# Late modulation blocks in the sample's small PSUM banks, and the sample's rows four partitions to a row

## The chip, the cores and the metric

The kernel runs on one core of one Trainium2 chip. The metric is device time in microseconds (us) of one execution, lower is better. Five engines work side by side: PE (TensorE, matrix products; PEld is its weight load), DVE (VectorE), ACT (ScalarE), POOL (GpSimd) and SP, whose queue issues nearly all direct DMAs here.

## The reference, cut to what matters

One inference step of a one-layer decoder over 512 prompt rows and 32 sample rows (8 sequences of 4). Both groups use the same weights:

```python
def adaln_mods(c, w_ada, b_ada):
    m = (jax.nn.silu(c) @ w_ada + b_ada)[:, None, :]
    return jnp.split(m, 6, axis=-1)

def finish(x, att, y_ssm, mods, g_att_out, w_out, g_norm2, ...):
    mixed = jnp.concatenate([rmsnorm(att, g_att_out), y_ssm], axis=-1) @ w_out
    x = x + mods[2] * mixed
    h = rmsnorm(x, g_norm2) * (1 + mods[4]) + mods[3]
    return x + mods[5] * hier_moe(h, w_rg, b_rg, w_re, b_re, w_gate, w_up, w_down)
```

`w_ada` is 1024 x 6144; its columns make the six modulations of 1024 columns each. Ahead of `finish` stand the input projection, three attention branches (compressed, selected, window) and a Mamba scan, each for prompt and sample. The model width is 1024; the mixture has 16 experts, two per row.

## The kernel before, in words

The kernel is written on a tile framework. A tile is taken from a pool by a tag; a tag has a fixed number of buffers, and a new tile of the tag takes the place of an older one once that one's readers are done. [...] `in_turn` (L360) only ties the PE instructions of the blocks that it wraps to one another, in the order in which they were traced.

The stage that the first half of the change touches is that of PSUM pool `pp2` (L850): tag `s` (scores, one pair of banks), `pt` (two banks; turns and evacuations of the prompt's attention), `ot` (one, attention output), `sm` (two) and `smo` (one) for the sample. In the order of the text:

- `win_half(0)`, compressed attention and top-k ranks of the sample, `sel_first(0)`: the first of two halves of selected attention for sample batches 0 to 3. `attend(t, br)` (L871) is attention of one prompt tile of 128 rows in branch `br`; it takes `s`, `pt` and `ot`. `attend(0, 1)`, `sel_second(0)`, `attend(1, 1)`, `win_half(1)` (L1240 to L1245).
- The sample's Mamba step, L1247 to L1362: turns, `hst` (the state) through four pairs of `sm` tiles (L1283 to L1294), `pe`, `pw_`, `pseg`, `py`, `pz`, and so on. Nearly every product goes to an `sm` bank.
- `sel_first(1)`, `attend(0, 0)`, `attend(2, 1)`, `sel_second(1)` (L1364 to L1367).
- The late blocks, L1377: `in_turn(ada_block, n, late_rows(n), "pt")` for n = 8 to 11. `ada_block` (L293) multiplies 512 columns of `w_ada` by the nine conditioning rows (32 columns of stationary data) into one bank, 64 PE records and 8 for the bias, and copies the bank to `mods`. `late_rows` (L1369) loads the block's 2 MB in two DMAs on SP's queue into the two buffers of tag `wt`, which `win_half(1)` used before. Then `store_mods(4, 8)` (L305) writes the four blocks to DRAM.
- `attend(3, 1)` (L1380), the prompt's compressed attention (L1382 to L1431, all of its PSUM tiles `pt`), `attend(1, 0)`, `attend(2, 0)`, `attend(3, 0)`.

The next stage (pool `pp3`, from L1456) turns the attention output (L1533), multiplies by `w_out` and keeps the 32 sample rows as 32 partitions x 1024 columns: `mixS`, `xs1`, and the three modulations `m0S`, `a2S`, `m3S`, each read back from DRAM (`mod_rowS`, L1505, a DMA that repeats every row four times). `samp_out` (L353) copies a bank of four 32-row blocks (partitions 32 j, columns 128 j) in four pieces to `mixS` (L1688). `sample_rows` (L1667) squares, norms, modulates, stores to `h2d` and runs the router in two halves (`router`, L1619). `OSEQ` (L30) is the order: 'm0 s f0 m1 r0 f1 m2 r1 f2 f3 m3 r2 r3', with s for `sample_rows`, m for a product tile of 128 prompt rows, f and r for its norm and router. After it come 17 expert tiles.

Of the kernel before, what the change touches and what calls it, by code (L numbers as in the profile page):

```python
# [9 lines left out]
F32 = mybir.dt.float32  # L10
# [9 lines left out]
KC = 8  # L20
# [30 lines left out]
def hybrid_step(ctx: ExitStack, tc: tile.TileContext, a, o):  # L51
# [21 lines left out]
    def W(pl, shape, dt, tag, bufs=2):  # L73
        return pl.tile(list(shape), dt, name=nm(tag), tag=tag, bufs=bufs)
# [10 lines left out]
    def PS(tag="ps"):  # L85
        return psum["pool"].tile([P, 512], F32, name=nm(tag), tag=tag, bufs=psum["tags"][tag])
# [7 lines left out]
    def mm(out, lhsT, rhs, start=True, stop=True):  # L94
        T.matmul(out, lhsT, rhs, start=start, stop=stop)  # L95
# [209 lines left out]
    def store_mods(n0, n1):  # L305
        for j in range(4):
            SP.dma_start(modd[:, n0:n1, j, :], mods[32 * j:32 * j + 9, n0:n1, :])
# [45 lines left out]
    def samp_out(ps, n, dst):  # L353
        for j in range((n + P - 1) // P):
            e = min(n, (j + 1) * P)
            dst(ps[32 * j:32 * j + 32, 0:e - j * P], j * P, e)
# [3 lines left out]
    def in_turn(f, *args):  # L360

        traced = nc.cur_bb.bb.instructions
        n0 = len(traced)
        r = f(*args)
        for i in traced[n0:]:
            if i.engine == mybir.EngineType.PE:
                if tail[0] is not None:
                    tc.add_manual_dep(i, tail[0].name, mybir.DependencyInfo(mybir.DependencyClass.NoSync,
                                                                            mybir.DependencyReason.DATA),
                                      reason="in_turn")  # L370
                tail[0] = i
        return r

    def proj(pl, H, L, lhs, w, n, dst, nb=2, ks=range(KC), between={}):

        acc = [PS("acc") for _ in range(NT)]
        ps = PS() if lhs is not None else None
        parts = {}  # L380
        turn = in_turn if between else lambda f, *args: f(*args)

        def prod(t, k):
            wh, wl = parts[k]
            sl = slice(t * P, (t + 1) * P)
            mm(acc[t][:, 0:n], H[:, k, sl], wh, start=k == ks[0], stop=False)
            mm(acc[t][:, 0:n], H[:, k, sl], wl, start=False, stop=False)
            mm(acc[t][:, 0:n], L[:, k, sl], wh, start=False, stop=k == ks[-1])

        for i, k in enumerate(ks):  # L390
            parts[k] = split_w(pl, w(k), n, nb)
            if i <= KC - nb:
                for t in range(NT):
                    turn(prod, t, k)
            if lhs is not None and i % 4 == 3:
                for j in ks[i - 3:i + 1]:
                    turn(samp_k, ps, lhs, w(j), n, j, ks)
            for f in between.get(k, ()):
                f()
        for t in range(NT):  # L400
            for k in ks[KC - nb + 1:]:
                turn(prod, t, k)
        if lhs is not None:
            samp_out(ps, n, dst)
        return acc

    def to_us(col):
# [359 lines left out]
    def CS(shape, dt, name):  # L767
        return smp.tile(list(shape), dt, name=name, tag=name)

    with tc.high_priority(offset=-2500):  # L770
# [33 lines left out]
                        teq[:, None, None, :].to_broadcast([P, 2, 8, 4]), op=OP.mult)  # L804
        X4 = CS([64, 64, 4], BF, "X4")
        V.tensor_copy(X4, ident[0:64, 0:64, None].to_broadcast([64, 64, 4]))
        sel32 = CS([P, 32], F32, "sel32")
        V.tensor_reduce(sel32, ident.rearrange("p (j r) -> p r j", r=32), axis=AX.X, op=OP.add)
        Eb = CS([P, 32, 8], BF, "Eb")
        V.tensor_copy(Eb, sel32[:, :, None].to_broadcast([P, 32, 8]))  # L810
# [102 lines left out]
    def C3(shape, dt, name):  # L913
        return W(p3, shape, dt, name, 1)
# [181 lines left out]
    def sel_first(hb, gt):  # L1096
        mx0, sm0, po = sel_part(hb, 0, gt)
        mx0_ = W(p3, [P, 1], F32, "mx0")
        V.tensor_copy(mx0_, mx0)
        po0 = W(p3, [P, P], F32, "pdT")  # L1100
        V.tensor_copy(po0, po[:, 0:P])
        return mx0_, sm0, po0

    def sel_second(hb, gt, mx0_, sm0, po0):
        mx1, sm1, po1 = sel_part(hb, 1, gt)
        mn = W(p3, [P, 1], F32, "mxm")
        V.tensor_tensor(mn, mx0_, mx1, op=OP.min)
        e0 = W(p3, [P, 1], F32, "e0")
        S.activation(e0, mx0_, AF.Exp, scale=-1.0, bias=mn)
        e1 = W(p3, [P, 1], F32, "e1")  # L1110
        S.activation(e1, mx1, AF.Exp, scale=-1.0, bias=mn)
        V.tensor_mul(sm0, sm0, e0)
        V.scalar_tensor_tensor(sm0, sm1, e1, sm0, op0=OP.mult, op1=OP.add)
        cf = factor(hb, 1, sm0)
        V.tensor_mul(e0, e0, cf)
        V.tensor_mul(e1, e1, cf)
        add_rows(hb, po0, e0)
        add_rows(hb, po1, e1)
# [125 lines left out]
    attend(1, 1, True)  # L1244
    win_half(1, wt1)  # L1245

    dtaS = C3([NS, 8], F32, "dtaS")  # L1247
    V.tensor_mul(dtaS, dtS, nega[0:NS])

# [30 lines left out]
    for g in range(2):  # L1280
        for h in range(2):
            V.tensor_copy(Cb[64 * h:64 * h + 64, :, g, h, :], xcS[64 * g:64 * g + 64, 5])
    po = PS("smo")  # L1283
    for b2 in range(4):
        ps = PS("sm")
# [75 lines left out]
    r = rstd(ssyS, 512, "xs", 0.25)  # L1361
    V.tensor_scalar(y3, y3, r, 0.5, op0=OP.mult, op1=OP.mult)  # L1362

    first1 = sel_first(1, gt10)  # L1364
    attend(0, 0)
    attend(2, 1, True)
    sel_second(1, gt11, *first1)  # L1367

    def late_rows(n):  # L1369
        ts = []  # L1370
        for hf in range(2):
            t = W(p3, [P, 2, 4, 256], F32, "wt", 2).rearrange("p b i c -> p (b i c)").rearrange("p (k c) -> p k c", k=4)
            SP.dma_start(t, w_ada[:, 4 * hf:4 * hf + 4, n * 512:n * 512 + 512])
            ts.append(t)
        return lambda k: ts[k // 4][:, k % 4, :]

    for n in range(8, 12):  # L1377
        in_turn(ada_block, n, late_rows(n), "pt")
    store_mods(4, 8)
    attend(3, 1, True)  # L1380

    k3 = kcv[:, 0:P].rearrange("p (g d) -> p g d", d=64)  # L1382
# [2 lines left out]
    ps = PS("pt")  # L1385
    T.transpose(ps[:, 0:16], kcv[:, 0:P], ident[0:16, 0:16])

    kcT = W(p2, [P, 240], F32, "kcT", 1)
    V.memset(kcT, 0.0)
    for g in range(2):  # L1390
        gs = slice(64 * g, 64 * g + 64)
        V.tensor_scalar_mul(kcT[gs, 112 + 64 * g:128 + 64 * g], ps[gs, 0:16], gqc[gs])
    ps = PS("pt")
    mm(ps[:, 0:P], rep.rearrange("p h c -> p (h c)"), kcv[:, P:256])
    vblk = W(p2, [P, 2, 4, 64], F32, "vblk", 1)
# [2 lines left out]

    pcs = PS("pt")
    for q in range(4):  # L1400
        mm(pcs, kcT[:, 112 - 16 * q:240 - 16 * q], QT[:, q, :], start=q == 0, stop=q == 3)
    scT_ = W(p2, [P, 512], F32, "psb", 3)
    evac(scT_, pcs)
    psc = PS("pt")
# [27 lines left out]
    attend(1, 0)  # L1432
    attend(2, 0)
    attend(3, 0)

    RS = W(tl, [P, 2, 8, 32], F32, "RS", 1)
    V.tensor_tensor(RS, RTt.rearrange("p h b t -> p h (b t)")[:, :, None, :].to_broadcast([P, 2, 8, 32]),
# [52 lines left out]
        W(p6, shape, F32, tag, bufs)  # L1490
    catH = W(p6, [P, KC, 512], F32R, "catH", 1)
    catL = W(p6, [P, KC, 512], F32R, "catL", 1)
    xs1 = W(p6, [NS, D], F32, "xs1", 1)
    for shape, tag, bufs in (([P, 4, P], "h2T", 3), ([P, 512], "t512", 2), ([P, 1], "ssS", 1)):
        W(p6, shape, F32, tag, bufs)
    p6w, close_p6w = pool("p6w")
# [8 lines left out]
    def mod_rowS(n, m):  # L1505
        SP.dma_start(m, dram(modv, 4 * D + (n - 2) * D, [[4 * D, NB], [0, TS], [1, D]]))

    for i in range(3):
        mod_row(2 + i, M[:, i, :])
    m0S, a2S, m3S = [W(p6s, [NS, D], F32, "MS", 3) for _ in range(3)]  # L1510
    mod_rowS(2, m0S)
    mod_rowS(4, a2S)
    mod_rowS(3, m3S)
    g2 = W(p6, [P, D], F32, "h2")
    SP.dma_start(g2, dram(a["g_norm2"], 0, [[0, P], [1, D]]))
    mg = W(p6, [24, P], F32, "h2T", 3)
# [2 lines left out]
    SP.dma_start(mg[16:24, :], dram(a["g_norm2"], 0, [[P, 8], [1, P]]))  # L1519
    V.scalar_tensor_tensor(M[:, 2, :], M[:, 2, :], 1.0, g2, op0=OP.add, op1=OP.mult)  # L1520
    V.tensor_scalar_mul(M[:, 2, :], M[:, 2, :], -1.0 / 8192)
    V.scalar_tensor_tensor(a2S, a2S, 1.0, g2[0:NS], op0=OP.add, op1=OP.mult)
    V.tensor_scalar_mul(a2S, a2S, -1.0 / 8192)
    SP.dma_start(x1, a["x_prompt"].rearrange("o (t p) d -> p (o t) d", p=P))
    SP.dma_start(xs1, a["x_sample"].rearrange("b t d -> (b t) d"))

    ko = (4, 5, 6, 7, 0, 1, 2, 3)
    for k in ko:
# [136 lines left out]
                                   og[0:n, t, :, None].to_broadcast([n, 4, 4]), op0=OP.is_lt, op1=OP.mult)  # L1665

    def sample_rows():  # L1667
        h2 = W(p6s, [NS, D], F32, "h2S", 1)
        ss = W(p6, [NS, 1], F32, "ss2")
        S.activation(h2, xs1, AF.Square, accum_out=ss)  # L1670
        x = W(p6, [NS, 1], F32, "ms2")
        V.tensor_scalar(x, ss, 1.0 / D, EPS, op0=OP.mult, op1=OP.add)
        r = rsqrt_col(x, "h2s")
        V.scalar_tensor_tensor(h2, xs1, r, a2S, op0=OP.mult, op1=OP.mult)
        V.tensor_add(h2, h2, m3S)
        SP.dma_start(h2d[512:512 + NS, :], h2)
        lgS = lg[0:NS, 4, :]
        V.tensor_tensor(lgS, router(h2, NS, wr, 0), rb[0:NS], op=OP.add)
        V.tensor_tensor(lgS, router(h2, NS, wr, 1), lgS, op=OP.add)
        rank(4)  # L1680

    mixS = W(p6s, [NS, D], F32, "h2S", 1)
    w0 = load_w(w_out, 0, 512, "wout", (1, 0))
    w1 = load_w(w_out, 512, 512, "wout", (1, 0))

    def to_mix(n):
        def f(src, c0, c1):
            S.copy(mixS[:, 512 * n + c0:512 * n + c1], src)  # L1688
        return f

    wL = [SLOT([P, 4, 512], F32R, "wL") for _ in range(2)]
    acc = proj(p6u, catH, catL, catS, w0, 512, to_mix(0), ks=ko)
    close_p6u()
    pw2["u"], close_pwu = pool("pwu", "right")
    ms = W(p6, [P, NT], F32, "ms", 1)
# [11 lines left out]
    load_part(2, 2, 0)  # L1707
    load_part(2, 2, 2)
    early("u")
    samp_out(ps, 512, to_mix(1))  # L1710
    V.tensor_mul(mixS, mixS, m0S)
    V.tensor_add(xs1, xs1, mixS)
    SP.dma_start(xsd, xs1)

    h2s = {}

# [471 lines left out]
```

## Time and profile before

| what | value |
|---|---|
| median of 3 runs | 811.96 us (806.91 to 815.54) |
| profiled execution | 813.91 us |
| its span in the trace | 812.2 us |
| mean granted clock of PE | 0.908 of full speed |
| PE busy | 714.6 us, 88% |
| DVE busy | 492.2 us, 61% |
| ACT busy | 348.4 us, 43% |

The profiled execution took 1.7 us more than its span, which begins and ends with the first and last instruction. [...] A group of instructions is read as line, engine, operation, output <- inputs, shapes, count. "x" after a busy time counts instructions; a product of 32-bit data shows as two records of PE.

### The profile page before, as it was taken

How to read it: one execution, taken by the hardware profiler on the slowest of the kernel's cores; microseconds unless marked ns; L12 is line 12 of the kernel's file. 1: busy time of each engine (PE TensorE's matmuls, PEld its weight loads, DVE VectorE, ACT ScalarE, POOL GpSimd, SP SyncE). 2: the span in 40 equal slices, each digit the busy share in tenths (PEclk: the TensorE clock that was granted, in tenths of full speed). 3: DMA queues.
4: the chain of work that ended last, by engine and by line, in shares of the span. 5: the costliest groups of instructions: out<-in, count | busy, mean ns of one | idle time of the engine just before them, and what ended most of it. 6: DMA issues, size and time to landing. Idle time of an engine off the chain costs nothing. (4 is left out here: it accounts for less than half of the span.)

```text
span 812.2 us, 14470 instructions
## 1 busy us (share of the span) xinstructions
PE 714.6 (88%) x5484; PEld 519.0 (64%) x5484; DVE 492.2 (61%) x1302; ACT 348.4 (43%) x799; POOL 142.1 (17%) x165
## 2 busy tenths in 40 slices
PE   4999999899897999659989788899948999999993
PEld 3677877777674766437456365678835676667662
DVE  7443783526529774354324644758996797887773
ACT  3324444425234435311133344623433575677671
POOL 3012021231313101012000100003131222224221
PEclk9999999899996979865599899999859999999997
DMA  8954885054474661482635310748858899998311
GB/s 287 391 128 154 297 307 205 2 189 151 180 272 164 233 232 46 163 311 104 196 122 206 112 45 1 235 156 285 323 175 339 247 311 338 316 335 281 85 22 26
DMA packets 67259, 161.86 MB, mean 199 GB/s; under 512 B 19171, under 2 KB 31404, under 8 KB 60788
## 3 DMA queue, kind: packets, MB, share of 16 engines
q1 hardware_dynamic: 56964, 115.54, 40.8%
q0 software_dynamic: 10224, 45.37, 16.6%
q8 instruction: 44, 0.72, 0.4%
q14 instruction: 27, 0.22, 0.1%
HBM read 153.48 MB, written 20.74 MB: 215 GB/s over the span
## 5 line engine op out<-in xcount | busy, mean ns | idle before, releaser
L892 ACT ACTIVATE psb<-s,amx 128x128 f32<-128x128 f32 (+3 forms) x64 | 33.2, 523 | 53.4 <-DVE amx L888 26.2
L95 PE MATMUL acc<-wh,hH 128*128 128x512 f32 (+1 forms) x128 | 49.2, 385 | 0.5 <-PE acc L95 0.5
L95 PE MATMUL acc<-wl,hH 128*128 128x512 f32 (+1 forms) x128 | 47.6, 372 | 0.0
L95 PE MATMUL acc<-wh,hL 128*128 128x512 f32 (+1 forms) x128 | 47.4, 370 | 0.0
L95 PE MATMUL acc<-gu,XF 128*128 128x512 f32 x88 | 46.5, 611 | 0.0
L95 PE MATMUL acc<-wh,XH 128*128 128x512 f32 x68 | 44.5, 655 | 0.4 <-ACT XH L1954 0.4
L344 DVE TENSOR_TENSOR wl<-dn,wh 128x512 fp32r<-128x512 f32 x52 | 34.1, 686 | 8.3 <-ACT wh L343 8.2
L895 PE MATMUL pt<-ident,psb 128*128 128x128 f32 x160 | 30.3, 298 | 10.0 <-ACT psb L892 9.4
L105 ACT COPY kt<-sm 128x512 f32<-128x512 f32 x33 | 19.0, 586 | 41.6 <-PE sm L1036 31.1
L344 DVE TENSOR_TENSOR wl<-gu,wh 128x512 fp32r<-128x512 f32 x44 | 29.6, 688 | 10.4 <-ACT wh L343 8.8
L343 ACT CAST wh<-dn 128x512 fp32r<-128x512 f32 x52 | 30.8, 619 | 10.7 <-PE acc L95 8.8
L2003 POOL DMA_INDIRECT out_y_prompt<-yo,gi x13 | 21.2, 1629 | 76.7 <-DVE gi L1923 16.8
L95 PE MATMUL acc<-wh,HH 128*128 128x512 f32 x68 | 32.3, 478 | 2.1 <-ACT HH L1986 2.1
L1071 POOL DMA_INDIRECT gsel<-in_cache_sel,idx x16 | 16.0, 1001 | 100.2 <-PE smo L95 71.2
L343 ACT CAST wh<-gu 128x512 fp32r<-128x512 f32 x44 | 26.2, 619 | 16.7 <-PE acc L95 10.3
L895 PEld LDWEIGHTS pt<-ident,psb 128*128 128x128 f32 x160 | 18.9, 150 | 19.0 <-ACT psb L892 14.8
L1724 POOL TENSOR_TENSOR h<-x,M 128x512 f32<-128x512 f32 x4 | 8.8, 2214 | 122.6 <-DVE x L1699 94.2
L95 PE MATMUL s<-KT,QT 64*128 64x384 f32 (+3 forms) x128 | 29.3, 521 | 0.8 <-ACT KT L863 0.8
L888 DVE TENSOR_REDUCE amx<-s 128x1 f32<-128x384 f32 (+1 forms) x32 | 18.5, 619 | 18.8 <-PE s L95 18.8
L95 PE MATMUL acc<-wl,XH 128*128 128x512 f32 x68 | 29.1, 427 | 0.8 <-DVE wl L344 0.8
L95 PE MATMUL ps<-wada,scT 128*32 128x128 f32 x512 | 27.8, 282 | 1.5 <-DVE modT L433 1.0
L95 PE MATMUL acc<-wl,HH 128*128 128x512 f32 x68 | 29.0, 427 | 0.0
(783 smaller groups left out, 1922.1 us busy)
## 6 DMA issues: line engine op xcount, KB each, us to landing
wada<-in_w_ada SPq DMA_DIRECT2D x16, 1024.0 KB
dn<-in_w_down SPq DMA_DIRECT2D x12, 1024.0 KB
gu<-in_w_gate SPq DMA_DIRECT2D x21, 512.0 KB
gu<-in_w_up SPq DMA_DIRECT2D x21, 512.0 KB
wt<-in_w_ada SPq DMA_DIRECT2D x8, 1024.0 KB
gux<-in_w_gate SPq DMA_DIRECT2D x11, 512.0 KB
gux<-in_w_up SPq DMA_DIRECT2D x11, 512.0 KB
wt<-in_cache_win SPq DMA_DIRECT2D x4, 1024.0 KB
```

The source lines that it names most:

```text
L95: T.matmul(out, lhsT, rhs, start=start, stop=stop)
L105: S.copy(out, in_)
L343: S.copy(wh[:, 0:n], w)
L344: (eng or V).tensor_sub(wl[:, 0:n], w, wh[:, 0:n].bitcast(F32))
L888: V.tensor_reduce(mx[:, g:g + 1], s2[:, g, 0:n], axis=AX.X, op=OP.max, negate=True)
L892: S.activation(pb[:, 0:n], s2[:, g, 0:n], AF.Exp, bias=mx[:, g:g + 1], accum_out=sm[:, h:h + 1])
L895: T.transpose(pt[:, c * P:(c + 1) * P], pb[:, c * P:(c + 1) * P], ident)
L1071: G.indirect_dma_start(out=t.rearrange("p r c -> p (r c)"), out_offset=None, in_=sel_rows, in_offset=bass.IndirectOffsetOnAxis(ap=idx[:, 2 ...
L1724: G.tensor_mul(h2s[t][:, 0:512], x1[:, t, 0:512], M[:, 2, 0:512])
L2003: G.indirect_dma_start(out=y_p, out_offset=bass.IndirectOffsetOnAxis(ap=gi, axis=0), in_=yo, in_offset=None, bounds_check=511, oob_is_err= ...
```

## The change

Two edits. First, the four late blocks go to tag `sm` in place of `pt`, and to other places of the text: n = 8 ahead of the turns of `hst`, n = 9 ahead of `sel_first(1)`, n = 10 behind it, n = 11 behind `sel_second(1)`. `late_rows` moves up with them. Second, the sample's rows are held as 128 partitions x 2 x 128 columns: partition 32 j + r holds columns 128 j and 512 + 128 j of row r. The modulations come from `mods` by a product with a 0/1 matrix (`pick`) in place of three DMAs from DRAM; the row sum of squares is completed by a product with `same4`; loads and stores of these rows become four DMAs each; the turn for the router is two 128 x 128 turns.

```diff
@@ proj
-        if lhs is not None:
+        if lhs is not None and callable(dst):
             samp_out(ps, n, dst)
+        elif lhs is not None:
+            S.copy(dst, ps[:, 0:P])
@@ sample, Mamba step and selected attention
+    in_turn(ada_block, 8, late_rows(8), "sm")
     po = PS("smo")
     for b2 in range(4):
         ps = PS("sm")
...
+    in_turn(ada_block, 9, late_rows(9), "sm")
     first1 = sel_first(1, gt10)
+    in_turn(ada_block, 10, late_rows(10), "sm")
     attend(0, 0)
     attend(2, 1, True)
     sel_second(1, gt11, *first1)
-    for n in range(8, 12):
-        in_turn(ada_block, n, late_rows(n), "pt")
+    in_turn(ada_block, 11, late_rows(11), "sm")
     store_mods(4, 8)
     attend(3, 1, True)
@@ prompt, compressed attention: kcT 240 -> 176 columns, its offsets 64 less
@@ after attend(3, 0)
+    pick = W(p3, [P, P], F32, "pdT").rearrange("p (j b t) -> p j b t", j=4, b=NB)
+    V.tensor_copy(pick, ident.rearrange("p (j r) -> p j r", r=32)[:, :, 1:9, None].to_broadcast([P, 4, NB, TS]))
+    SMt = tl.tile([P, 6, P], F32, name="SMt")
+    for n0, n1 in ((0, 4), (4, 6)):
+        ps = PS("sm")
+        mm(ps[:, 0:P * (n1 - n0)], pick.rearrange("p j b t -> p (j b t)"), mods[:, n0:n1, :].rearrange("p n c -> p (n c)"))
+        S.copy(SMt[:, n0:n1, :].rearrange("p n c -> p (n c)"), ps[:, 0:P * (n1 - n0)])
@@ stage of the out-projection
-    m0S, a2S, m3S = [W(p6s, [NS, D], F32, "MS", 3) for _ in range(3)]
-    mod_rowS(2, m0S)
-    mod_rowS(4, a2S)
-    mod_rowS(3, m3S)
+    SM4 = W(p6s, [P, 6, P], F32, "SM4", 1)
+    S.copy(SM4, SMt)
+    m0S, m3S, a2S = SM4[:, 0:2], SM4[:, 2:4], SM4[:, 4:6]
+    g24 = W(p6s, [P, 2, P], F32, "g24", 1)
+    for j in range(4):
+        SP.dma_start(g24[32 * j:32 * j + 32], dram(a["g_norm2"], j * P, [[0, NS], [512, 2], [1, P]]))
+    same4 = W(p6s, [P, 4, NS], F32, "same4", 1)
+    V.tensor_copy(same4, sel32[:, None, :].to_broadcast([P, 4, NS]))
...
-    V.scalar_tensor_tensor(a2S, a2S, 1.0, g2[0:NS], op0=OP.add, op1=OP.mult)
+    V.scalar_tensor_tensor(a2S, a2S, 1.0, g24, op0=OP.add, op1=OP.mult)
...
-    SP.dma_start(xs1, a["x_sample"].rearrange("b t d -> (b t) d"))
+    for j in range(4):
+        SP.dma_start(xs1[32 * j:32 * j + 32], dram(a["x_sample"], j * P, [[D, NS], [512, 2], [1, P]]))
@@ sample_rows
-        h2 = W(p6s, [NS, D], F32, "h2S", 1)
+        h2 = W(p6s, [P, 2, P], F32, "h2S4", 1)
         S.activation(h2, xs1, AF.Square, accum_out=ss)
+        ps = PS("pr")
+        mm(ps[:, 0:1], same4.rearrange("p j r -> p (j r)"), ss)
...
-        SP.dma_start(h2d[512:512 + NS, :], h2)
+        for j in range(4):
+            SP.dma_start(h2d[512:512 + NS, :].rearrange("r (h j c) -> j r h c", h=2, j=4)[j], h2[32 * j:32 * j + 32])
-        V.tensor_tensor(lgS, router(h2, NS, wr, 0), rb[0:NS], op=OP.add)
-        V.tensor_tensor(lgS, router(h2, NS, wr, 1), lgS, op=OP.add)
+        with tc.high_priority(offset=100):
+            pt = PS()
+            for hf in range(2):
+                T.transpose(pt[:, hf * P:hf * P + P], h2[:, hf, :], ident)
+            hT = W(p6, [P, 2, 4, NS], F32, "h2T", 3)
+            evac(hT.rearrange("p h j r -> p (h j r)"), pt[:, 0:2 * P])
+            pr = PS("pr")
+            for k in range(KC):
+                mm(pr[0:NS, 0:20], hT[:, k // 4, k % 4, :], wr[:, k, :], start=k == 0, stop=k == KC - 1)
+            V.tensor_tensor(lgS, pr[0:NS, 0:20], rb[0:NS], op=OP.add)
@@ out-projection
-    mixS = W(p6s, [NS, D], F32, "h2S", 1)
+    mixS = W(p6s, [P, 2, P], F32, "mixS", 1)
-    acc = proj(p6u, catH, catL, catS, w0, 512, to_mix(0), ks=ko)
+    acc = proj(p6u, catH, catL, catS, w0, 512, mixS[:, 0], ks=ko)
...
-    samp_out(ps, 512, to_mix(1))
+    S.copy(mixS[:, 1], ps[:, 0:P])
     V.tensor_mul(mixS, mixS, m0S)
     V.tensor_add(xs1, xs1, mixS)
-    SP.dma_start(xsd, xs1)
+    for j in range(4):
+        SP.dma_start(xsd.rearrange("r (h j c) -> j r h c", h=2, j=4)[j], xs1[32 * j:32 * j + 32])
```

## Rows read from the trace of the kernel before

**Rows 1.** the page: busy us (share of the span), instructions, by engine.

```profile
PE 714.6 (88%) x5484; PEld 519.0 (64%) x5484; DVE 492.2 (61%) x1302; ACT 348.4 (43%) x799; POOL 142.1 (17%) x165
```

**Rows 2.** busy time by stretch: us, engines (instructions), granted clock, DMA.

```profile
320.00:360.00 40.00, 24.29 (x247) 15.89 (x236) 17.69 (x57) 11.79 (x30) 6.60 (x7) 0.82 0.62 238
360.00:400.00 40.00, 38.10 (x288) 25.00 (x291) 18.17 (x45) 4.84 (x12) 4.94 (x4) 0.54 0.43 142
400.00:420.00 20.00, 16.12 (x201) 10.20 (x197) 3.83 (x8) 6.23 (x14) 0.96 (x1) 0.82 0.59 189
420.00:460.00 40.00, 34.24 (x318) 24.20 (x310) 19.51 (x58) 14.11 (x33) 4.12 (x16) 0.91 0.29 108
460.00:510.00 50.00, 43.50 (x288) 29.18 (x286) 23.49 (x46) 22.86 (x66) 0.00 (x0) 1.00 0.17 64
...
540.00:580.00 40.00, 39.76 (x327) 32.65 (x326) 30.89 (x78) 11.61 (x32) 7.52 (x3) 1.00 0.88 310
580.00:600.00 20.00, 10.35 (x110) 9.90 (x110) 19.16 (x82) 8.99 (x14) 3.76 (x5) 0.62 0.53 199
```

**Rows 3.** busy time of instructions on the score tile s alone.

```profile
327.00:419.00 92.00, 0.00 (x0) 0.00 (x0) 0.47 (x3) 0.00 (x0) 0.68 0.53 187
```

**Rows 4.** timeline of PE: start us, us, operation, [idle before <-releaser].

```profile
322.70 1.13 PE L95 MATMUL s<-KT,QT 64*128 64x512 f32 x4
...
363.72 1.92 PE L95 MATMUL pt<-wt,scT 128*32 128x128 f32 x28
...
413.79 3.44 PE L95 MATMUL pt<-wt,scT 128*32 128x128 f32 x64 [3.00 <-DMA wt<-in_w_ada]
...
418.55 0.66 PE L895 MATMUL pt<-ident,psb 128*128 128x128 f32 x4
```

**Rows 5.** tile pt, 316 to 425 us: ns min/median/max, first and last start.

```profile
L95 PE MATMUL pt<-wt,scT x256: 272/421/423, 363.7 to 416.8; 128*32 128x128 f32 x128
...
L303 ACT COPY mods<-pt x4: 266/266/272, 377.0 to 418.8; 128x128 f32<-128x128 f32 x4
```

**Rows 6.** tile wt: issues of the weight loads of the late blocks.

```profile
L1373 SPq DMA_DIRECT2D wt<-in_w_ada x8: 367/368/448, 354.4 to 405.5; - x8
```

**Rows 7.** busy time by stretch, attention beside the sample.

```profile
260.00:320.00 60.00, 57.17 (x490) 40.79 (x489) 41.86 (x121) 28.42 (x94) 7.35 (x8) 0.85 0.44 159
```

**Rows 8.** timeline: 512-column products of the prompt.

```profile
444.00 3.67 PE L95 MATMUL pt<-QT,kcT 128*128 128x512 f32 x8
```

**Rows 9.** timeline: last product of the sample, first instructions of the next stage.

```profile
458.82 0.42 PE L95 MATMUL smo<-selnew,snT 32*32 32x128 f32 x8
...
510.51 1.04 PE L1533 MATMUL ps<-ident,zy 128*128 128x128 f32 x8
```

**Rows 10.** timeline of PE, two sample halves: first and last product of each.

```profile
297.22 1.11 PE L1036 MATMUL sm<-ident,gsel 128*128 128x128 f32 x4
...
318.29 1.95 PE L95 MATMUL smo<-gsel,kt 128*32 128x128 f32 x64
...
328.22 1.48 PE L1036 MATMUL sm<-ident,gsel 128*128 128x128 f32 x8 [3.73 <-DMA gsel<-in_cache_sel,idx]
...
344.38 0.42 PE L95 MATMUL smo<-selnew,snT 32*32 32x128 f32 x8
```

**Rows 11.** tile h2S: duration ns min/median/max, first and last start.

```profile
L1688 ACT COPY h2S<-ps x8: 256/258/261, 547.7 to 552.4; 32x128 f32<-32x128 f32 x8
...
L1711 DVE TENSOR_TENSOR h2S<-h2S,MS x1: 1207/1207/1207, 553.4 to 553.4; 32x1024 f32<-32x1024 f32 x1
...
L1674 DVE SCALAR_TENSOR_TENSOR h2S<-xs,rsq_zh2s,MS x1: 1274/1274/1274, 561.4 to 561.4; 32x1024 f32<-32x1024 f32 x1
```

**Rows 12.** groups by line: busy us, mean ns of one | idle before.

```profile
L105 ACT COPY kt<-sm 128x512 f32<-128x512 f32 x33 | 19.0, 586 | 41.6 <-PE sm L1036 31.1 <-PE sm L1288 10.4
...
L1974 DVE SCALAR_TENSOR_TENSOR th<-th,wt,acc 128x256 f32<-128x256 f32 x17 | 8.1, 479 | 0.4
```

**Rows 13.** timeline, 500 to 548 us: the sample gate and what it waited for.

```profile
526.73 1.21 DVE L1522 SCALAR_TENSOR_TENSOR MS<-MS,h 32x1024 f32<-32x1024 f32 x1 [1.87 <-DMA MS<-modd]
```

More of the change, by code (lines that the diff above doesn't have):

```diff
@@ L806, in hybrid_step @@
         V.tensor_copy(X4, ident[0:64, 0:64, None].to_broadcast([64, 64, 4]))
-        sel32 = CS([P, 32], F32, "sel32")
+        sel32 = const([P, 32], F32, "sel32")
         V.tensor_reduce(sel32, ident.rearrange("p (j r) -> p r j", r=32), axis=AX.X, op=OP.add)
@@ L1245, in hybrid_step, with late_rows @@
     win_half(1, wt1)
+    def late_rows(n):
+        ts = []
+        for hf in range(2):
+            t = W(p3, [P, 2, 4, 256], F32, "wt", 2).rearrange("p b i c -> p (b i c)").rearrange("p (k c) -> p k c", k=4)
+            SP.dma_start(t, w_ada[:, 4 * hf:4 * hf + 4, n * 512:n * 512 + 512])
+            ts.append(t)
+        return lambda k: ts[k // 4][:, k % 4, :]
     dtaS = C3([NS, 8], F32, "dtaS")
@@ L1367, in hybrid_step @@
     sel_second(1, gt11, *first1)
[L1369 to L1375, printed above, removed]
-    for n in range(8, 12):
-        in_turn(ada_block, n, late_rows(n), "pt")
+    in_turn(ada_block, 11, late_rows(11), "sm")
     store_mods(4, 8)
@@ L1386, in hybrid_step @@
     T.transpose(ps[:, 0:16], kcv[:, 0:P], ident[0:16, 0:16])
-    kcT = W(p2, [P, 240], F32, "kcT", 1)
+    kcT = W(p2, [P, 176], F32, "kcT", 1)
     V.memset(kcT, 0.0)
@@ L1391, in hybrid_step @@
         gs = slice(64 * g, 64 * g + 64)
-        V.tensor_scalar_mul(kcT[gs, 112 + 64 * g:128 + 64 * g], ps[gs, 0:16], gqc[gs])
+        V.tensor_scalar_mul(kcT[gs, 48 + 64 * g:64 + 64 * g], ps[gs, 0:16], gqc[gs])
     ps = PS("pt")
@@ L1400, in hybrid_step @@
     for q in range(4):
-        mm(pcs, kcT[:, 112 - 16 * q:240 - 16 * q], QT[:, q, :], start=q == 0, stop=q == 3)
+        mm(pcs, kcT[:, 48 - 16 * q:176 - 16 * q], QT[:, q, :], start=q == 0, stop=q == 3)
     scT_ = W(p2, [P, 512], F32, "psb", 3)
@@ L1492, in hybrid_step @@
     catL = W(p6, [P, KC, 512], F32R, "catL", 1)
-    xs1 = W(p6, [NS, D], F32, "xs1", 1)
+    xs1 = W(p6, [P, 2, P], F32, "xs1", 1)
     for shape, tag, bufs in (([P, 4, P], "h2T", 3), ([P, 512], "t512", 2), ([P, 1], "ssS", 1)):
@@ L1667, in sample_rows @@
     def sample_rows():
-        h2 = W(p6s, [NS, D], F32, "h2S", 1)
-        ss = W(p6, [NS, 1], F32, "ss2")
+        h2 = W(p6s, [P, 2, P], F32, "h2S4", 1)
+        ss = W(p6, [P, 1], F32, "ss2")
         S.activation(h2, xs1, AF.Square, accum_out=ss)
-        x = W(p6, [NS, 1], F32, "ms2")
-        V.tensor_scalar(x, ss, 1.0 / D, EPS, op0=OP.mult, op1=OP.add)
+        ps = PS("pr")
+        mm(ps[:, 0:1], same4.rearrange("p j r -> p (j r)"), ss)
+        x = W(p6, [P, 1], F32, "ms2")
+        V.tensor_scalar(x, ps[:, 0:1], 1.0 / D, EPS, op0=OP.mult, op1=OP.add)
         r = rsqrt_col(x, "h2s")
@@ L1675, in sample_rows @@
         V.tensor_add(h2, h2, m3S)
-        SP.dma_start(h2d[512:512 + NS, :], h2)
+        for j in range(4):
+            SP.dma_start(h2d[512:512 + NS, :].rearrange("r (h j c) -> j r h c", h=2, j=4)[j], h2[32 * j:32 * j + 32])
         lgS = lg[0:NS, 4, :]
-        V.tensor_tensor(lgS, router(h2, NS, wr, 0), rb[0:NS], op=OP.add)
-        V.tensor_tensor(lgS, router(h2, NS, wr, 1), lgS, op=OP.add)
+        with tc.high_priority(offset=100):
+            pt = PS()
+            for hf in range(2):
+                T.transpose(pt[:, hf * P:hf * P + P], h2[:, hf, :], ident)
[5 more added lines that the diff above has]
+            V.tensor_tensor(lgS, pr[0:NS, 0:20], rb[0:NS], op=OP.add)
         rank(4)
-    mixS = W(p6s, [NS, D], F32, "h2S", 1)
+    mixS = W(p6s, [P, 2, P], F32, "mixS", 1)
     w0 = load_w(w_out, 0, 512, "wout", (1, 0))
     w1 = load_w(w_out, 512, 512, "wout", (1, 0))
[L1686 to L1689, printed above, removed]
     wL = [SLOT([P, 4, 512], F32R, "wL") for _ in range(2)]
-    acc = proj(p6u, catH, catL, catS, w0, 512, to_mix(0), ks=ko)
+    acc = proj(p6u, catH, catL, catS, w0, 512, mixS[:, 0], ks=ko)
     close_p6u()
```

## The prediction, made before the changed kernel was run

> **What bounds the kernel now.** I read the page first: PE is busy 88% of the span, more than any other engine [rows 1]; the chain of waits that ended last covers only the tail and says nothing of the middle. So I went to busy time by stretch [rows 2]. [...] The whole from 320 to 510 holds, as busy time times clock, 24.29 x 0.82 + 38.10 x 0.54 + 16.12 x 0.82 + 34.24 x 0.91 + 43.50 = 128.4 us of PE work at full clock in 190 us, or 0.68 us per us.
>
> Why is work left for 460 to 510 that PE had room for at 323? The score tile answers [rows 3]: between 327 and 419 us PE does nothing on `s`, so prompt attention stands still for 92 us. The timeline says where: the scores of `attend(3, 1)` run at 322.70, and its first turn into `pt` comes at 418.55, directly behind the last late block, whose 64 products begin at 413.79 [rows 4]. The late blocks own the `pt` banks from 363.7 to 418.8 [rows 5]; they come before `attend(3, 1)` in the text, there are two such banks, and a later tile can't pass them. Block 11 in turn waited 3.00 us for its weights [rows 4], which are loaded two halves at a time from 354.4 to 405.5 [rows 6], as `wt` comes free. So the prompt waits for weights that wait for the sample.
>
> **First half of the change, the banks.** Taken away: the late blocks on `pt`. `attend(3, 1)`, the compressed attention and the last three `attend` have no other input from the sample, so they can fill PE from 323 us on, as the earlier `attend` calls did. How dense does PE get when they do? There are three rows to choose from. From 260 to 320, attention beside the sample, it is 57.17 x 0.85 = 48.6 in 60 us, 0.81 [rows 7]; from 420 to 460, the same mix, 34.24 x 0.91 / 40 = 0.78 [rows 2]; attention alone, 460 to 510, gives 0.87. Below, the present 0.68 is the bound if nothing mixes. I take 0.80, between the two that are the same mix.
>
> Added work: the block products are the same in number. The two products with `pick` have 512 and 256 columns; eight records (four products) of 512 columns took 3.67 us [rows 8], so 0.92 + 0.46 = 1.4 us. The stage needs (128.4 + 1.4) / 0.80 = 162 us, so it ends at 482 and not at 510: 28 us less. At 0.87 it is 149 us (41 less), at 0.78 166 us (24 less), at 0.68 191 us (none less).
>
> Can the sample keep up? Its last product ends at 459.2 [rows 9], and from 360 to 420 much of its time is PE at the low clock. With full clock those 40 us hold 20.6 us of work, so there is slack for the turns that attention takes. Both bodies of work then end near each other, which is why I use the density of PE and not either chain alone.
>
> What is moved with it: eight weight DMAs on SP's queue. The first pair goes out when `win_half(1)` frees `wt`, as now, and its block starts 363.72 - 354.4 = 9.3 us later [rows 4, 6]. In front of it stands the sample's Mamba start, so most of this is covered; blocks 9 to 11 get a stretch of the Mamba step or a half of selected attention, 17 to 23 us [rows 10], to load in, more than the 9.3. Behind block 8 wait the turns of `hst`, which share two `sm` banks with it; bounds 0 and 9.3 us on the sample's chain, and I take it as inside the density. `store_mods(4, 8)` moves from 419 to the end of the stage: the three modulation loads wait for it on SP's queue, and what is queued behind them is the load of the residual rows and `g_norm2`, then DVE's first product with them. No row here shows such a late store; below it is 0, above the 1.87 us that DVE now waits for a load from the same tensor [rows 13]. I take +1.
>
> [...]
>
> **Second half, the rows.** DVE: five two-operand instructions of 32 x 1024 (three of 1.207, one of 1.274, one of 1.211 us [rows 11, 13]) become 128 x 256. The nearest row of that size is 0.479 us [rows 12]: 6.1 - 2.4 = 3.7 us less. Added are two copies of 128 x 128, under 0.479 each, in part in the stage before. ACT: eight copies of 0.258 [rows 11] become two of about 0.266 [rows 5], 1.5 us less; the copy `SM4` of 768 columns costs between one and two of 512 columns (0.586 [rows 12]), say 0.9 more, and the copies behind `pick` 1.0 in the stage before. SP issues 16 small DMAs where it issued six. The norm gains a step over PE and back.
>
> What of it is on the path? From 540 to 580 PE is the bound (39.76 of 40) and DVE's saving there is worth nothing by itself; its backlog is the bound from 580 to 600 [rows 2], and less backlog enters. Earlier, DVE's wait of 1.87 us for the repeated-row DMA [rows 13] goes, in favour of four short loads. So the whole lies between -5.6 (3.7 + 1.87, all of it on the path) and +3 (`SM4`, the hop over PE and the DMA issues all on the path, nothing gained). I take -3, near the lower end, since the 20 us are DVE's alone.
>
> **Sum.** 813.9 (the profiled execution) - 28 - 3 + 1 = 784. It lies 1.9 above the median of the runs shown, so in medians 782.
>
> **Rivals.** (a) *The clock stays low.* From 360 to 400 PE was busy 38.10 of 40 us and yet had 0.54 [rows 2]; if that stretch stays as it is, 20.6 us of work in 40, and the rest runs at 0.80, the stage takes 40 + (129.8 - 20.6) / 0.80 = 176 us, 14 less: 797 in medians. Against it: between 260 and 320, with attention in between, the clock was 0.85 [rows 7]. [...]
>
> (b) *Attention fits in wholly* and the stage runs as dense as attention alone, 0.87: 41 less, 769. For it: ACT and DVE are busy under half of 320 to 420 [rows 2]. Against: no mixed stretch did it.
>
> [...]
>
> (d) *The sample's chain becomes the bound.* Attention takes turns on PE, ACT and DVE between its steps, and its two `sm` banks are lent to the late blocks. One half of selected attention took 23.0 us beside attention (297.22 to 320.24) and 16.6 alone (328.22 to 344.80) [rows 10], 1.39 times. The chain from 323 to 459.2 is 136 us; 1.39 times that, with block 11 (3.9 us) and the `pick` step (1.4 on PE, 1.0 on ACT) now behind it, ends at 323 + 189 + 6 = 518 against 510.5 [rows 9], 8 us later: 813.9 + 8 - 3 + 1 = 820, 818 in medians, slower than before. It decides from 1.33 times on. Against: much of that chain, 360 to 400, is PE at the lower clock, which would be relieved, and its last 40 us already ran beside attention.
>
> **How the numbers follow.** My sum 0.42, (b) 0.20, (a) 0.18, (c) 0.10, (d) 0.10. The point is the sum's, 782; its own range is 772 to 792 (774 to 786 by a density of 0.84 to 0.78, and the second half at its bounds, -5.6 and +3 for the -3). The range that should hold 8 in 10 takes in (a), the bulk of (b) and part of (c): 764 to 806. About 1% (8 us) is what a measurement of this kernel can tell from no change. Faster by more: the sum, (a) and (b), 0.80. Within: (c) and 0.04 of (d), 0.14. Slower by more: the rest of (d), 0.06.
>
> **What would show it.** Right: PE has products on `s` all through 327 to 419; the stage of the out-projection begins between 475 and 492; the granted clock between 360 and 400 is over 0.75; busy time on `sm` includes the late blocks; 32 x 1024 rows are gone and the stretch before the first expert is a few us shorter from its own start. Wrong: `s` still pauses (c); it does not pause, but the sample's last product ends past 500 (d); the clock stays near 0.5 while PE is busy (a). I am wrong in the second half if DVE has less to do and the time from the out-projection's start to the first expert's products is not shorter.

## The result, and the profile after

The changed kernel took 777.17 us (median of 4 runs, 770.00 to 782.99) against 813.75 for the kernel before beside it (4 runs): a ratio of 0.955, 95% interval 0.942 to 0.967, so 36.6 us less. The prediction said 782 within 764 to 806, faster. Two later sets of the same kernel gave 774.5 and 771.5 us (6 runs each, ratios 0.948 and 0.949 to their own runs of before). Ratios leave out executions that are over 1.5% slower than the fastest of the same kernel; the profile of one experiment, new banks in the old place, is of such an execution. The profiled execution of the changed kernel took 774.86 us, with a span of 773.1.

The profile after in the stretches of [rows 2], us, engines, granted clock, DMA:

```profile
320.00:360.00 40.00, 39.19 (x372) 27.35 (x370) 21.56 (x54) 19.05 (x48) 3.94 (x5) 1.00 0.31 106
360.00:400.00 40.00, 35.82 (x293) 25.86 (x293) 21.43 (x59) 11.03 (x34) 7.97 (x8) 0.74 0.57 211
400.00:420.00 20.00, 20.00 (x174) 13.60 (x171) 13.19 (x40) 5.54 (x16) 0.00 (x0) 0.83 0.26 56
420.00:460.00 40.00, 39.15 (x406) 29.05 (x409) 20.10 (x42) 21.71 (x53) 1.92 (x2) 1.00 0.60 228
```

From 320 to 360 PE is busy 39.19 us where it was busy 24.29, at 1.00 where it had 0.82; from 360 to 400 the clock is 0.74 where it was 0.54. The score tile alone, in the stretch of [rows 3]:

```profile
327.00:419.00 92.00, 12.86 (x54) 3.73 (x36) 8.94 (x16) 11.04 (x36) 0.85 0.42 147
```

The late blocks' products on the tile `wt`, which answer to [rows 5]:

```profile
L95 PE MATMUL sm<-wt,scT x256: 269/273/423, 379.1 to 471.8; 128*32 128x128 f32 x128
```

Where PE had no product on `s`, it now has 54 records of products. The median record of a late block takes 273 ns and not 421. Beside the first block (379.1 to 381.1 us) the granted clock was 1.00 and its 64 records have a median of 273; beside the first 32 records of the first block before (363 to 371 us) it was 0.50, with a median of 421. No block waited for its weights in this profile.

The end of the stage and the start of the next, [rows 9] before, on PE's timeline:

```profile
474.17 1.09 PE L1553 MATMUL ps<-ident,zy 128*128 128x128 f32 x8 [0.24 <-ACT SMt L1448]
...
479.91 0.50 PE L95 MATMUL acc<-wh,catH 128*128 128x512 f32 x1 [2.74 <-ACT catH L1554]
...
564.75 1.12 PE L1977 MATMUL ps<-ident,xg 128*128 128x128 f32 x4 [1.80 <-DMA xg<-h2d,gir]
```

I split the span at three marks: the first scores of prompt attention (251.59 before, 256.43 after), the first transpose of the out-projection (510.51, 474.17) and the first gathered row of the experts (601.35, 564.75). Up to the first mark the profile after is 4.8 us later; attention with the sample takes 217.7 instead of 258.9, 41.2 less; the out-projection to the experts 90.6 instead of 90.8; the rest 208.4 instead of 210.9. Sum: +4.8 - 41.2 - 0.3 - 2.5 = -39.2, the difference of the spans. Three things to explain: why 41 and not 28, why the rows gave nothing, and the 4.8 us in a part that the change doesn't touch.

### The profile page after: what moved, and what is told of

Its sections match the earlier page's. It is cut to its first block, busy times and chain, and to the rows that moved or that the text cites. A ratio compares the mean times of both kernels' runs of the same rounds, so it can differ in the third digit from the quotient of the medians.

```text
span 773.1 us, 14455 instructions
## 1 busy us (share of the span) xinstructions
PE 702.6 (91%) x5484; PEld 520.9 (67%) x5484; DVE 486.8 (63%) x1303; ACT 346.1 (45%) x795; POOL 143.5 (19%) x165
## 5 line engine op out<-in xcount | busy, mean ns | idle before, releaser
L95 PE MATMUL s<-KT,QT 64*128 64x384 f32 (+3 forms) x128 | 31.1, 535 | 0.8 <-ACT KT L865 0.8
L95 PE MATMUL ps<-wada,scT 128*32 128x128 f32 x512 | 29.5, 301 | 1.9 <-DVE modT L435 1.9
L2024 DVE TENSOR_TENSOR yo<-acc,M 128x512 f32<-128x512 f32 x34 | 23.1, 687 | 10.6 <-PE acc L95 10.5
L95 PEld LDWEIGHTS acc<-wh,hH 128*128 128x128 f32 x128 | 24.2, 189 | 7.3 <-issue 3.3
L95 PEld LDWEIGHTS ps<-wada,scT 128*32 128x32 f32 x512 | 23.0, 121 | 7.3 <-issue 2.6
```

Of the source, the lines that this page charges most:

```text
L2024: V.tensor_tensor(yo[:, cols], po, M5[:, cols], op=OP.mult)
```

## The experiments

Each set was run beside the kernel before on the same chip; ratios are to that. Of each change only the core of the diff stands.

**The change again** (no edit), twice, for its profile.

> The changed kernel itself, run beside the parts of it. Every theory: 777 us within 5, and a ratio to the kernel before of 0.955. It is here for a second profile: if the 5 us by which the first profile is later than the kernel before at 320 us came from that one execution, they are gone (the first scores of prompt attention at 251 to 253 us, where they were in the kernel before, not at 256); if they belong to the change, they are there again.

Measured: 774.5, ratio 0.948 (0.944 to 0.953); first scores at 255.5. So the late start was there again. The other time:

> The changed kernel itself once more, as the measure for the three beside it on the same chip: 770 to 780 by every theory.

Measured: 771.5, ratio 0.949 (0.944 to 0.955); first scores at 251.5, as in the kernel before. One program, two starts. What differs is the granted clock (last but two) between 215 and 225 us, first in the one profile, then in the other:

```profile
215.00:220.00 5.00, 4.22 (x19) 3.20 (x19) 1.88 (x6) 1.11 (x2) 0.00 (x0) 0.50 0.00 0
220.00:225.00 5.00, 5.00 (x78) 3.72 (x77) 2.13 (x5) 0.18 (x1) 2.93 (x3) 0.50 0.02 3
```

```profile
215.00:220.00 5.00, 3.80 (x68) 2.99 (x70) 3.42 (x9) 1.11 (x2) 0.52 (x1) 1.00 0.01 3
220.00:225.00 5.00, 5.00 (x54) 3.90 (x43) 2.18 (x10) 0.88 (x3) 4.27 (x4) 1.00 0.22 28
```

So the 4 to 5 us at the start are no part of the change.

**The banks alone.** The kernel before, with

```
+    in_turn(ada_block, 8, late_rows(8), "sm")     # before the state step
+    in_turn(ada_block, 9, late_rows(9), "sm")     # before sel_first
+    in_turn(ada_block, 10, late_rows(10), "sm")   # behind sel_first
+    in_turn(ada_block, 11, late_rows(11), "sm")   # behind sel_second
-    for n in range(8, 12):
-        in_turn(ada_block, n, late_rows(n), "pt")
```

> The change without its second half: late blocks on the sample's banks at their new places, the rows as in the kernel before (32 partitions, repeated-row loads of the modulation). Theory, by the two traces: the banks bring everything, so this runs within 2 us of the whole change, 775 to 781. By the prediction's sum the rows are worth 3 us: 780. By its lower bound for the rows, 5.6: 783. If the store of the modulation at the end of the stage hurts more where the sample's rows are loaded from it too (three loads more behind it), up to 2 us more than each of these. If the rows were the reason of the gain: 810.

Measured: 773.6, ratio 0.950 (0.946 to 0.954), as the whole change beside it (0.948, 0.944 to 0.953). The banks and places bring all of it. On the score tile, in the stretch of [rows 3], there is no pause:

```profile
327.00:419.00 92.00, 11.73 (x48) 3.45 (x32) 7.67 (x15) 11.04 (x36) 0.80 0.37 128
```

**The rows alone.** The changed kernel with the loop over `"pt"` in its old place.

> The other half alone: rows four partitions to a row, the late blocks on the banks of prompt attention at their old place. Theory: the rows are worth nothing, since PE is the bound for 50 us of the stage and the copies on ACT stand in front of the first product: 812 to 816, ratio 0.995 to 1.005. By the prediction's sum 811, ratio 0.996; by its bounds 808 to 817. Prompt attention's pause on the score tile, 92 us long, is there as in the kernel before, by every theory that blames the banks.

Measured: 815.4, ratio 1.001 (0.998 to 1.005): no difference. On the score tile, over 100 us:

```profile
328.00:428.00 100.00, 0.00 (x0) 0.00 (x0) 1.46 (x5) 1.56 (x4) 0.66 0.53 184
```

The pause is there as in [rows 3].

**New places, old banks.** The changed kernel with `"pt"` for `"sm"` in its four calls.

> The whole change, but the four late blocks keep prompt attention's banks at their new places in the text. Theory (the banks decide): attention has to wait for the last block on its banks, and as the blocks now stand in front of two more of the attention calls, more of it is behind them: the pause on the score tile is there again, 80 to 110 us long, and the time is that of the kernel before or above, 812 to 850. Rival (the place decides: blocks spread between the sample's steps hide their loads, whatever bank they use): 777 to 785, and no pause over 30 us.

Measured: 818.7, ratio 1.005 (1.002 to 1.009): no faster, and at most a little slower than before (816.1 beside it). The score tile again, and behind it PE's timeline at the first block:

```profile
287.00:395.00 108.00, 0.00 (x0) 0.00 (x0) 0.87 (x4) 0.46 (x2) 0.70 0.53 184
```

```profile
356.53 3.47 PE L95 MATMUL pt<-wt,scT 128*32 128x128 f32 x64
```

Attention stands still for 108 us, and the first block is on `pt` at 356.53, earlier than in [rows 4]. Places without the banks gain nothing.

**New banks, old place.** The changed kernel with the loop in its old place, on `"sm"`.

> The whole change, but the four late blocks stand at their old place in the text (one behind the other, after the sample's selected attention) and only their banks are the sample's. Theory (the banks free attention, the places hide the loads): attention runs on as in the changed kernel and has its last product by about 460, but the four blocks come at the very end of the sample's chain; the first has its weights, each of the other three waits about 9 us for two loads that start when the block before has released them, so the stage ends 18 to 25 us later than in the changed kernel: 790 to 800. Rival (the banks alone do it, the place is worth nothing): 772 to 780.

Measured: 806.6, ratio 0.986 (0.980 to 0.991). The profiled execution took 816.0, so its lines are read for the order and the waits:

```profile
485.47 3.40 PE L95 MATMUL sm<-wt,scT 128*32 128x128 f32 x64 [13.89 <-DMA wt<-in_w_ada]
...
496.39 3.64 PE L95 MATMUL sm<-wt,scT 128*32 128x128 f32 x64 [7.17 <-DMA wt<-in_w_ada]
...
507.14 3.64 PE L95 MATMUL sm<-wt,scT 128*32 128x128 f32 x64 [6.53 <-DMA wt<-in_w_ada]
...
513.62 1.09 PE L1551 MATMUL ps<-ident,zy 128*128 128x128 f32 x8 [0.24 <-ACT SMt L1446]
```

Attention isn't held (48 records on the score tile from 327 to 419), but in this execution three blocks wait 27.6 us in all for their loads with nothing beside them, and their products run at a granted clock of 0.55, 0.50 and 0.50 (3.40, 3.64 and 3.64 us where the first block of the changed kernel, at 1.00, takes 1.96). I had expected 790 to 800, from about 9 us for each of the three waits: the waits add up to that, the time came out longer. During the first wait nothing but transfers runs, at 375 GB/s (last column; the share before it is of 16 DMA engines):

```profile
472.00:485.00 13.00, 0.00 (x0) 0.00 (x0) 0.00 (x0) 0.00 (x0) 0.00 (x0) 0.61 0.98 375
```

The two loads go out at 470.74 and 472.53, among those of the next stages' weights, with which they share this traffic. So the banks are worth 12 us by themselves (806.6 against 818.1 beside it), the places nothing, and both together 42 (773.6 against 816.1).

**The store cut in two.** The changed kernel with

```
     in_turn(ada_block, 9, late_rows(9), "sm")
+    store_mods(4, 6)
...
-    store_mods(4, 8)
+    store_mods(6, 8)
```

> The changed kernel with the store of the late modulation cut in two: the rows that the out-projection needs (blocks 4 to 9) are stored right behind block 9, some 50 us earlier, and only blocks 10 and 11 at the end of the stage. The wait of 3.28 us of DVE for the loads at 489 us goes, and the three loads of M go out about 4 us earlier. If that wait lies on the path (the prediction's +1 for the late store, or more): 772 to 774. If PE, which is busy without a pause from 484 on, hides it: as the changed kernel within 1 us, 773 to 776.

Measured: 772.7, ratio 0.945 (0.941 to 0.948), not to be told from the changed kernel. The late store cost nothing: the wait that it made in the profile after is on DVE,

```profile
489.00 1.23 DVE L1539 SCALAR_TENSOR_TENSOR M<-M,h 128x1024 f32<-128x1024 f32 x1 [3.28 <-DMA h<-in_g_norm]
```

longer than the 1.87 us of [rows 13], while PE was busy without a pause from 484 to 540.

**Blocks one place earlier.** That edit, and block 9 in the middle of the state step, 10 and 11 at the places of 9 and 10.

> The last run's edit, and blocks 9, 10 and 11 each one place earlier among the sample's steps (9 in the middle of the state step), so that no late block is behind the sample's selected attention. Taken from the end of the stage: block 11, 3.8 us of PE between 468.6 and 472.4. Theory: the sample's chain ends the stage, so about 4 us less than the run before: 768 to 771. Rival: the sum of PE's work ends the stage and the blocks are only moved: 772 to 776. Against both: block 9 waits 9 us for its weights at its new place and holds the sample's chain: 778 to 784.

Measured: 770.3, ratio 0.944 (0.939 to 0.950): the median is lower, the intervals overlap. The stage with attention was not 4 us shorter: 217.2 us, where the changed kernel had 217.7, 217.7 and 217.3. So taking block 11 off the end did not visibly do what I expected of it; but the run with only the store cut had 223.9 in its profile, so that single profiles hardly settle 4 us in this stage. What was shorter is the next stretch, 88.7 us (below).

**DVE's saving taken back**, tried twice: five products of 32 x 1024 with nothing to do with the result, at the places of [rows 11, 13].

> The changed kernel with DVE's saving taken back: five products of 32 x 1024 of zeros with themselves (about 1.2 us each, 6 us) at the places where the kernel before had its five instructions of that size. Theory (DVE's time is not on the path between the out-projection and the experts): 774 to 776, as the changed kernel. The prediction's step (from 580 to 600 DVE's backlog is the bound): 777 to 780.

Measured: 775.6, ratio 0.949 (0.944 to 0.953). This run says nothing: its products waited for nothing, and all ran between 462.9 and 470.7 us, in the stage before. So each was tied to a value of its place:

```
+    V.scalar_tensor_tensor(dm, dm, mixS[0:NS, 0, 0:1], dm, op0=OP.mult, op1=OP.mult)
```

> The changed kernel with DVE's saving taken back, this time at the places themselves: five products of 32 x 1024 (about 1.2 us each, 6 us), each with a scalar from the row it stands behind, so that none can run before it. In the last such run all five ran between 462 and 471 us, before the out-projection, and said nothing. Theory (DVE is not what ends the stretch from the out-projection to the experts): the changed kernel within 1.5 us, and 90 to 92 us from the first transpose of the out-projection to the first gathered row at PE. The prediction's step (DVE's backlog is the bound behind PE): 3 to 4 us more in both.

Measured: 778.5, ratio 0.955 (0.951 to 0.960), beside 0.949 (0.944 to 0.955) of the changed kernel: higher, intervals overlapping. In the profile the five take 7.3 us (one of them 2.20) and the stretch from the first transpose of the out-projection to the gathered row 92.7 us, where the changed kernel has 90.6, 91.5 and 90.1. So in this one profile, which is of the fastest of the six executions (772.74), 7.3 us of DVE cost 1 to 3 us there. The medians lie 7.0 apart, and their intervals leave anything from nothing to more than the whole 7.3 open: how much of DVE's time lies on the path, this run does not settle.

**Two things more, and the old rows at the best places.**

> The earlier stores and places of the run before last, and two things more: the products with pick move from the end of the stage to behind block 11 (in that run they stood between the last products of the sample for 1.9 us, at 464.44), and the copy SM4 goes from ACT to POOL, which is idle (on ACT it stands for 0.83 us in front of catH, for which PE waits). Theory (the sample's chain ends the stage and ACT's copies delay the next): 2 to 3 us less than the run before last, 766 to 769. Rival (PE's whole work ends both stages): as that run, 769 to 772.

Measured: 771.3, ratio 0.945 (0.940 to 0.950), no better than the run whose places it has. The last:

> The earlier stores and places with the rows of the kernel before: no products with pick, no copies of their results, three repeated-row loads instead. Theory (the rows are worth nothing): 769 to 772, as the run with the same places and the new rows. If the pick products at the end of the chain cost what they take there: 767 to 769. By the prediction's step (rows worth 3): 773 to 775.

Measured: 767.1, ratio 0.942 (0.937 to 0.947): the lowest median of all, with the rows of the kernel before. Against the changed kernel beside it (0.949, 0.944 to 0.955) the intervals still overlap, so it is the best candidate and not a proven gain over it.

## Why the prediction was right, and where not

**The diagnosis held.** `s` has products all through 327 to 419, and the runs bear out its cause: with the blocks on `pt` the pause is there, whatever the rows (815.4) and whatever the places (818.7); with the blocks on `sm` it is gone, at the new places (773.6) and at the old one (806.6).

**The first half's -28 was mis-sized: it was -41** (and -41.6 in the profile with the early start, 258.9 to 217.3). The step is "the stage needs 162 us". In the same way of reckoning, busy time times clock, the stretch from 325.0 (320 and the 4.8 us of lateness) to 474.2 holds 124.7 us of work in 149.2: a density of 0.84 and not 0.80, and less work than the 129.8 that I had carried over. At 0.80 that work would take 155.9, so of the 13 us that were missing some 6 are work and some 7 density. Busy time by clock is thus no constant of the work: for the same products, and the two with `pick` more, 4 us less of it were counted. Why, no run tells. The stage of the out-projection began at 474.17, 473.27 and 468.80, just before the 475 to 492 that I had asked for.

The density is also not the same in each execution. With the same banks and places, the stage took 222.0 us in the profile of the banks alone, 223.9 with the store cut and 225.6 in the first run with products put back on DVE: 33 to 37 less than before and not 41. There the clock from 400 to 420 was 0.57, 0.57 and 0.66 where the first profile of the change has 0.83. The banks alone:

```profile
400.00:420.00 20.00, 20.00 (x130) 12.59 (x129) 9.08 (x25) 4.54 (x14) 0.97 (x1) 0.57 0.34 83
```

In the same reckoning the banks alone hold 121.3 us of work from 320 to 473.15, a density of 0.79. So the work was less than I had carried over in either case; the higher density is that of some executions, and whether the edits or the execution decide it, no run tells.

The result lies between my sum, 782, and rival (b), 769. That it came within 5 us of the sum is partly luck: in the first profile the 13 us that the first half gave beyond its term stand against 3 that the rows did not give and 4.8 of the late start. The two later sets lie 7.5 and 10.5 below the sum.

**Moving the loads was rightly costed at nothing, but the place mattered more than the prediction said.** The banks alone gave 12 us, since a block that has no other work beside it waits for its loads in full. At the new places no block waited. In the run with the old place blocks whose weights were late left PE idle, 27.6 us in all. Attention was done by then, so whether a late block would have held it up as well is not shown.

**The store's +1 was 0**: the wait came (3.28 us on DVE), and PE's work hid it.

**The second half's -3 was 0.** The step that failed is that the 20 us of [rows 2] are DVE's alone, so that what is saved there counts. With the rows alone, the 20 us that answer to 580 to 600 (586.63 to 606.63) have DVE busy 17.36 us and not 19.16: DVE now waits for PE's router products, 0.75 us in this line and 0.49 in another, where it had no wait between 580 and 594 before.

```profile
594.91 0.18 DVE L1770 TENSOR_TENSOR lg<-pr,lg 128x20 f32<-128x20 f32 x1 [0.75 <-PE pr L95]
```

And the last 8 us, from PE's last product with `Ab` to the gathered row, are a chain from product to DVE, back and to a DMA that the rows don't touch: 7.91 us before, 7.77 with the rows alone. Split at the first product with `catH`, the stretch from the first transpose to the gathered row (us, from the profiles) is:

| | to the first `catH` product | from there | sum |
|---|---|---|---|
| before | 3.51 | 87.33 | 90.84 |
| rows alone | 4.25 | 86.84 | 91.09 |
| banks and places alone | 6.22 | 84.66 | 90.88 |
| the change, three profiles | 5.74 each | 84.84, 85.71, 84.35 | 90.58, 91.45, 90.09 |
| DVE's saving taken back | 5.73 | 86.97 | 92.70 |
| blocks earlier, new rows | 4.01 | 84.64 | 88.65 |
| blocks earlier, old rows | 2.93 | 84.93 | 87.86 |

The rows alone take 0.5 off the second part and add 0.7 to the first: nothing. The second part does get 1.6 to 3.0 shorter, but by the first half of the change, with old rows as with new ones: when the stage opens, attention is done. Before, its last results were late, and PE waited four times in the first 20 us, 4.2 us in all: 1.87 and 0.48 for weights that DVE and ACT split into a high and a low part, 1.20 and 0.67 for attention's last output. Two of these waits on the timeline of the kernel before:

```profile
524.04 0.51 PE L95 MATMUL acc<-wl,catH 128*128 128x512 f32 x1 [1.87 <-DVE wl L344]
...
530.17 1.53 PE L1533 MATMUL ps<-ident,qa 128*128 128x128 f32 x8 [1.20 <-DVE qa L1445]
```

In the same stretch the banks alone leave one wait of 0.72, the first profile of the change none. And the first part gets 2.2 to 2.7 longer, again with either rows, because casts of weights now stand on ACT in front of `catH`. The changed kernel, ACT's timeline:

```profile
473.53 0.86 ACT L1448 COPY SMt<-sm 128x512 f32<-128x512 f32 x2 [0.76 <-PE sm L95]
474.27 4.26 ACT L1730 CAST wH<-wout 128x512 fp32r<-128x512 f32 x8
478.44 0.83 ACT L1526 COPY SM<-SMt 128x768 f32<-128x768 f32 x1
479.17 1.27 ACT L1554 ACTIVATE catH<-ps,gcat 128x512 fp32r<-128x512 f32 x2
```

In the run of the banks alone half of these casts wait 3.00 us more for the load of `wout`. The run with earlier blocks and old rows:

```profile
466.02 2.18 ACT L1707 CAST wH<-wout 128x512 fp32r<-128x512 f32 x4
469.87 1.26 ACT L1537 ACTIVATE catH<-ps,gcat 128x512 fp32r<-128x512 f32 x2 [1.67 <-PE ps L1536]
473.83 2.18 ACT L1707 CAST wH<-wout 128x512 fp32r<-128x512 f32 x4 [2.70 <-DMA wout<-in_w_out]
```

Before, `catH` came at 511.15, 0.64 us behind the first transpose, and the eight casts behind the first two of it. Here half of them run while PE still does the sample, and PE has its first product after 2.93 us. I had priced `SM4` (0.83 measured, 0.9 said) and not the casts, which the change doesn't touch but whose order it changes. That the 2 to 3 us by which the two runs with earlier blocks are shorter in this stretch come from here is read off the table; why the casts came to stand there was not tested by itself.

**The rivals.** (a), the clock that stays low, was half right: 360 to 400 had 0.74 and not the "over 0.75" that I asked for, and the stage was fast all the same. How full PE is does not tell the clock here: from 320 to 360 PE was busy 39.19 of 40 us and had 1.00, from 360 to 400 it was busy 35.82 of 40 us at 0.74, and in the line of the banks alone above 20.00 of 20 us at 0.57. What sets it, no run tells. (c), a score tile that still pauses, did not come: from 327 to 419 it has 54 records of products. (d) has the right mechanism and the wrong price: attention's last product ends at 458.6 and the sample's chain is what ends the stage, with PE idle in it,

```profile
465.35 0.39 PE L1030 MATMUL sm<-ident,sn 128*32 128x128 f32 x1 [4.58 <-ACT sn L1028]
```

but at 474 and not at 518: from 327.8 to the end of the sample's last product at 470.4 the chain took 143 us, late blocks included, where it was 136, far under the 1.33 times from which it decides.

## What to carry to other kernels

When two independent bodies of work share PE, look for the tile of the one that stands still, and for what holds its banks: late work of one body on the banks of the other makes the other stand still for as long as it takes (92 us here). Move the work to banks of the body that it belongs to and also between steps that hide its loads; here the first alone gave 12 us, the second alone nothing, both together 42. And when a stage ends earlier, look at what the next stage's engines have queued at its start: here the casts in front of `catH` ate some 2 us of what came free.

## What the runs showed of the hardware that was not expected

The granted clock can differ for several microseconds between two executions of one program at the same instructions: 0.50 from 215 to 225 us in one, 1.00 in the other, with the same waits of 1.44 and 0.78 us about it, and 4 us of span. In the profiles of all kernels here the first scores come either at 250.6 to 251.6 us or at 255.2 to 256.4, with nothing between. The stage with attention, too, took from 216.8 to 225.6 us with the same banks at the change's places, with a clock from 400 to 420 between 0.57 and 0.91; what of that is due to the kernels' other edits, no run tells. So one profile against another is worth no more than some 5 us, in this stage 8, and parts of a change of that size have to be read from several profiles of a stretch between two marks, or from medians.

These products on PE take not quite twice the time at half the clock. The first profile of the changed kernel and the one with the early start show it on the 64 records of one early block, first at 0.50, then at 1.00, 3.64 us against 1.95, which is 1.87 times:

```profile
221.34 3.64 PE L95 MATMUL ps<-wada,scT 128*32 128x128 f32 x64
```

```profile
218.73 1.95 PE L95 MATMUL ps<-wada,scT 128*32 128x128 f32 x64 [0.42 <-DVE ts L687]
```
